# A hybrid encoder block on one core: FFN sums kept in PSUM, weights split once, a planner that ranks by due time

## The chip, the cores and the metric

The kernel runs on one core of one Trainium2 chip. The metric is device time in microseconds (us) of one execution, as a median of several runs. Five engines work side by side, each through its own list of instructions in order: PE (matmul; PEld is its weight load), DVE (elementwise and reductions), ACT (activations, copies), POOL (elementwise on SBUF) and SP, which here issues the DMA transfers.

## The reference

One layer with 1024 tokens of width 1024, in f32: a SwiGLU FFN of inner width 2816, a token mixer, and a second FFN, each behind an RMSNorm that a conditioning vector modulates.

```python
x = x + 0.5 * g1 * swiglu(mod1(rms(x)), w1, w3, w2)
h = mod2(rms(x))
z = h @ w_in        # 8 heads of forget attention (q,k,v), 8 sparse query heads, index scores, gates
ya = fox_attention(...)                  # causal softmax with a cumulated forget bias
yb = dsa_attention(...)                  # softmax over the 256 best keys of each query by the index scores
x = x + g2 * ((sigmoid(ga) * (ya @ w_br_fox) + sigmoid(gb) * (yb @ w_br_dsa)) @ w_out)
x = x + 0.5 * g3 * swiglu(mod3(rms(x)), w1', w3', w2')
```

## The kernel before

**Arithmetic.** Every f32 matrix is split into a rounded high part and a low remainder (`wh`, `wl` of a weight, made by an ACT copy and a DVE or POOL subtraction), and each block product is three matmuls (`mm3`, line 390): high by high, high by low, low by high. A matmul takes 128 rows by 128 columns of weights and up to 512 columns of data.

**The FFNs.** Each is computed by a scheme with seven block products in place of eight (quarters a11, a12, a21, a22 of a weight, b11 to b22 of the data, and sums s1 to s4 and t1 to t4 of them). In the way up, `UpPair` (line 1417) takes one of 11 pairs of 256 inner columns; `steps` runs seven products for m = 0 (w1) and m = 1 (w3), one per `yield`. `product` (1457) splits a weight, takes a PSUM bank of 512 columns, and issues 12 matmuls. The seven products are put together by DVE: tile `u` or `v` in SBUF plus the PSUM bank (`plus`, line 1475), 14 such adds a pair. Then come SiLU on ACT, the multiplication, the sums t1 to t4 of the result for the second half, and stores of seven operands to `d_g` in DRAM. `up_all` (1528) sets the order: the first products of `head` pairs, then pair after pair, and between steps loads, weight sums and the conditioning matrices (`extra`). In the way down, `Down` (1568) runs the seven products over 11 blocks each with four banks, reading `d_g` back; `out` (1624) adds banks to the residual `xc` with `add`, a DVE operation, with `u` as an intermediate sum. There are eight banks, all of one pool (`bank`, bufs=8).

**The middle.** After the first FFN come a projection with `w_a`, the index scores, the exact top-k by bisection on DVE and ACT, while PE projects with `w_f` (forget attention's q, k, v), `w_q` (sparse queries) and `w_g` (gates, first half of the tokens); then attention of 16 heads with the gates of the second half beside it. `load_w` (496) loads a weight to a raw tile `wr` and splits it: ACT writes `wh`, POOL writes `wl`. The gates' weights are loaded and split twice, once for each half of the tokens. `Ring` (477) turns a few raw tiles and pairs in two pools, and `Ahead` (980) loads some pieces ahead. Then `branches`, `mixer_out` and the second FFN follow.

**The planner.** Nearly all of it is issued through `Plan` (163). `take` records each operation as a task with its dependencies and a rank: the place in program order plus `behind`. `flush` (264) then places tasks: on each engine it looks at the first 60 waiting tasks in order of rank and takes the one that could start first (a later one only if it starts over 0.05 us earlier), with durations from `length` (246), a result counted as 0.12 us late, one DMA wire of 345 GB/s, and a lock between DVE and POOL where both read SBUF (`t.port`). The instructions are then issued in the order of these planned starts, so each engine's list is fixed before the run. Tiles take a slot of their pool when their first task is placed.

Of the kernel before, what the change touches and what calls it, by code (L numbers as in the profile page):

```python
# [161 lines left out]

class Plan:
# [18 lines left out]
    def take(self, engine, op, a, kw):  # L182
# [31 lines left out]
        for j in before:  # L214
            self.tasks[j].after.append(t)
        t.left = len(before)
# [6 lines left out]
        t.port = engine in ("vector", "gpsimd") and "accum_out" not in kw and not any(  # L223
            v.tile.pool.space == PSUM for v in reads + writes)
# [21 lines left out]
    def length(self, t, e):  # L246
        if e == "tensor":
            if t.exact:
                return max(0.08, t.n / 2250.0)
            if t.op == "transpose":  # L250
                return t.n / 860.0
            return max(0.24, t.n / 500.0)
        more = "accum_out" in t.kw
        if e == "scalar":
            return 0.1 + t.n / 1200.0 + (0.3 if more else 0.12 if any(isinstance(t.kw.get(x), View) for x in ("bias", "scale")) else 0.0)
        if e == "vector":
            if t.op == "tensor_tensor_scan":
                return 0.1 + t.n / 450.0
            return max(0.2, 0.08 + t.n / 960.0 + (0.18 if more else 0.06 if t.op == "scalar_tensor_tensor" else 0.0))
        if e == "gpsimd":  # L260
            return 0.1 + t.n / (900.0 if t.op == "tensor_scalar" else 440.0)
        return 0.35

    def flush(self, keep=()):
# [6 lines left out]
        waiting = {e: [] for e in self.ENGINES}  # L271

        def release(t):
            insort(waiting[t.engine], t, key=lambda u: u.rank)
# [28 lines left out]
        while len(order) < len(tasks):  # L303
# [20 lines left out]
            d = self.length(t, e)  # L324
            end = s + d + 0.12
# [24 lines left out]
            for u in t.after:  # L350
                u.left -= 1
                u.ready = max(u.ready, s + d if u.engine == e and e != "sync" else end)
                if not u.left:
                    release(u)
# [35 lines left out]
def mm3(k, out, w_hi, w_lo, m_hi, m_lo, start, stop):  # L390
    mm = k.nc.tensor.matmul
    mm(out, w_hi, m_hi, start=start, stop=False)
    mm(out, w_hi, m_lo, start=False, stop=False)
    mm(out, w_lo, m_hi, start=False, stop=stop)
# [82 lines left out]
class Ring:  # L477
# [7 lines left out]
    def raw(self):  # L485
        p, n = self.raws[self.j % len(self.raws)]
        self.j += 1
        return p.tile([128, D], F32, tag="wr", name="wr", bufs=n)
# [6 lines left out]

def load_w(k, src, n):

    nc = k.nc
    raw = k.w.raw()
# [916 lines left out]

class UpPair:


    def __init__(self, k, i, w13, wq, bank, d_g, any_):  # L1420
# [3 lines left out]
        self.ahead = []  # L1424
# [28 lines left out]
    def block(self, ps, w, b, c):  # L1453
        s = slice(c * 128, c * 128 + 128)
        mm3(self.k, ps, w[0][:, s], w[1][:, s], *self.k.B[b][c], c == 0, c == 3)

    def product(self, src, b):
        w, ps = self.weight(src), self.bank()
        for c in range(4):
            self.block(ps, w, b, c)  # L1460
# [9 lines left out]
    def steps(self):  # L1470

        nc, tile, product, store = self.k.nc, self.tile, self.product, self.store
        u, v, z, g = [None, None], [None, None], {}, {}

        def plus(out, ps, t):
            nc.vector.tensor_add(out, ps, t)
            return out

        def result(m, j, t):

            if m == 0:
                z[j] = t
                nc.scalar.activation(t, t, AF.Silu)
            else:
                self.any.tensor_mul(t, t, z[j])
                g[j] = t
                if j != "b12":
                    store(j, t)
# [39 lines left out]
def up_all(k, pairs, head, order, steps, ahead, extra, eng, again=False, every=lambda n: n % 8):  # L1528
# [12 lines left out]
    for i, n in order:  # L1541
# [18 lines left out]
        if i >= 2 and len(order) - k.up_step < (PAIRS - 2) * 14 and every(k.up_step):  # L1560
            nc.behind = 150
            next(extra, None)
            nc.behind = 0
    stores(True)
# [3 lines left out]
class Down:  # L1568
# [5 lines left out]
             ("a21", "t1", None), ("a12", "b22", None))  # L1574
    LEAD = 6

    def __init__(self, k, s, w2, wq, bank, d_g, homes, x_in, done, any_):
        self.k, self.s, self.w2, self.wq, self.bank, self.d_g, self.done = k, s, w2, wq, bank, d_g, done
        self.a = {n: [None] * PAIRS for n in ("a11", "a12", "a21", "a22", "s2")}
        self.g, self.u, self.loaded = {}, {}, 0  # L1580
# [8 lines left out]
    def loads(self, upto):  # L1589

        while self.loaded < min(upto, 7 * PAIRS):
# [5 lines left out]
            for n, m in {0: [(q - 5, 0)] if q >= 5 else [], 2: [(q, 1)], 3: [(4 + q, 1), (4 + q, 0)]}.get(p, []):  # L1597
                if n < (4 if p < 3 else 8):
# [25 lines left out]
    def out(self, p, d, ps):  # L1624
# [5 lines left out]
        if p == 0:  # L1630
            u[d] = t512(self.k, name="u")
            nc.scalar.activation(u[d], ps, AF.Copy)
            add(0, 0, d, u[d])
# [3 lines left out]
        elif p == 2:  # L1637
            nc.vector.tensor_add(u[d], ps, u[d])
            add(0, 1, d, u[d])
        elif p == 3:  # L1640
            nc.vector.tensor_add(u[d], ps, u[d])
            add(1, 1, d, u[d])
            add(1, 0, d, u[d])
# [3 lines left out]
        elif p == 5:  # L1647
            add(0, 1, d, ps)
            add(1, 1, d, ps)
# [5 lines left out]
    def run(self, steps={}):  # L1655

        k = self.k
        for p, (first, _, early) in enumerate(self.ORDER):
            ps = [self.bank() for _ in range(4)]
# [619 lines left out]
```

## Time and profile before

| What | Value |
|---|---|
| runs before | 2259.95, 2266.53, 2271.02 us (median 2266.53) |
| profiled execution: span | 2259.4 us, 0.55 us under the fastest of the runs |
| busy: PE, DVE, ACT, POOL | 96%, 80%, 49%, 12% of the span |
| DMA | 315.89 MB, mean 140 GB/s |
| mean clock granted to PE | 0.989 of full |

The stages, by the names of the tiles in the trace: the first FFN's way up to about 479 us, its way down to about 708, the `w_a` projection to 746, index scores to 850, projections beside top-k to 1046, attention from 1052 to 1418, branches and output projection from 1428, the second FFN's products from about 1625 to the end. A busy PE in a profile contains the pipelined end of each matmul, so whether it runs at its pace is better read from the number of matmuls in a stretch than from its share of busy time.

### The profile page before, as it was taken

How to read it: one execution, taken by the hardware profiler on the slowest of the kernel's cores; microseconds unless marked ns; L12 is line 12 of the kernel's file. 1: busy time of each engine (PE TensorE's matmuls, PEld its weight loads, DVE VectorE, ACT ScalarE, POOL GpSimd, SP SyncE). 2: the span in 40 equal slices, each digit the busy share in tenths (PEclk: the TensorE clock that was granted, in tenths of full speed). 3: DMA queues.
4: the chain of work that ended last, by engine and by line, in shares of the span. 5: the costliest groups of instructions: out<-in, count | busy, mean ns of one | idle time of the engine just before them, and what ended most of it. 6: DMA issues, size and time to landing. Idle time of an engine off the chain costs nothing.

```text
span 2259.4 us, 31187 instructions
## 1 busy us (share of the span) xinstructions
PE 2178.7 (96%) x10508; PEld 1799.5 (80%) x10508; DVE 1802.3 (80%) x3391; ACT 1101.8 (49%) x1996; POOL 268.6 (12%) x255
## 2 busy tenths in 40 slices
PE   7999999999999999998999999899999999999999
PEld 5777888787887989996778887687888888888887
DVE  7998987889775488888788877668898877769765
ACT  4432232344464476787687787423443333324443
POOL 0000000000010223323555433000000000000000
PEclk9999999999999999999999999999999999999999
DMA  9234554497421313334332210767223442258520
GB/s 336 81 114 161 168 173 131 146 367 238 126 74 61 121 61 122 113 122 136 107 110 89 76 35 20 278 239 256 87 80 131 135 133 96 93 179 319 168 75 38
DMA packets 187421, 315.89 MB, mean 140 GB/s; under 512 B 27366, under 2 KB 51942, under 8 KB 187260
## 3 DMA queue, kind: packets, MB, share of 16 engines
q1 hardware_dynamic: 187260, 313.89, 41.1%
q8 instruction: 83, 1.36, 0.2%
q14 instruction: 78, 0.64, 0.1%
HBM read 237.53 MB, written 76.28 MB: 139 GB/s over the span
## 4 chain that ended last, share of the span: by engine, by line
PE 45%; DVE 3%; ACT 2%; DMA 2%; issue 1%; SPq 0%; ACTq 0%; DVEq 0%; POOL 0%
PE b L358 34%; PE py L358 6%; PE pt L358 3%; PE p L358 2%; DVE macc L358 1%; DMA wr<-in_w_g 1%; DMA mraw<-in_ada_w 0%; ACT pth L358 0%; ACT pr L358 0%; DVE ptl L358 0%; ACT kst L358 0%; DVE qs L358 0%; DMA wr<-in_wbr 0%; ACT yt L358 0%; DVE kst L358 0%
## 5 line engine op out<-in xcount | busy, mean ns | idle before, releaser
L358 PE MATMUL b<-h,wh 128*128 128x512 f32 x2720 | 855.8, 396 | 10.0 <-ACT wh L358 5.0
L358 PEld LDWEIGHTS b<-h,wh 128*128 128x128 f32 x2720 | 511.9, 189 | 136.1 <-ACT wh L358 9.1
L358 PE MATMUL b<-h,wl 128*128 128x512 f32 x1360 | 533.7, 395 | 2.4 <-DVE wl L358 2.4
L358 ACT ACTIVATE wh<-wr 128x512 fp32r<-128x512 f32 (+2 forms) x368 | 245.5, 676 | 469.3 <-PE b L358 343.8
L358 PEld LDWEIGHTS b<-h,wl 128*128 128x128 f32 x1360 | 256.2, 188 | 64.2 <-DVE wl L358 4.2
L358 DVE TENSOR_TENSOR z<-b,z 128x512 f32<-128x512 f32 x308 | 207.3, 684 | 73.0 <-PE b L358 71.9
L358 PE MATMUL b<-wl,wh 128*128 128x512 f32 x616 | 241.8, 393 | 5.5 <-DVE wl L358 5.5
L358 PE MATMUL b<-wh 128*128 128x512 f32 x616 | 239.4, 391 | 2.5 <-ACT wh L358 1.7
L358 PE MATMUL b<-wh,wl 128*128 128x512 f32 x616 | 241.2, 392 | 0.0
L358 DVE TENSOR_TENSOR wl<-wr,wh 128x512 fp32r<-128x512 f32 x312 | 206.7, 683 | 32.9 <-ACT wh L358 32.8
L358 PE MATMUL pj<-wh,h 128*128 128x384 f32 (+1 forms) x768 | 179.5, 319 | 0.1
L358 ACT ACTIVATE wh<-a 128x512 fp32r<-128x512 f32 x132 | 83.3, 631 | 194.0 <-PE b L358 168.3
L358 POOL TENSOR_TENSOR wl<-wr,wh 128x1024 fp32r<-128x1024 f32 (+2 forms) x56 | 120.1, 2150 | 283.8 <-ACT wh L358 276.9
L358 DVE TENSOR_TENSOR wl<-a,wh 128x512 fp32r<-128x512 f32 x132 | 91.4, 693 | 76.8 <-ACT wh L358 76.8
L358 PEld LDWEIGHTS b<-wl,wh 128*128 128x128 f32 x616 | 116.6, 189 | 31.9 <-DVE wl L358 7.6
L358 PEld LDWEIGHTS b<-wh 128*128 128x128 f32 x616 | 116.1, 188 | 27.8 <-ACT wh L358 2.3
L358 PEld LDWEIGHTS b<-wh,wl 128*128 128x128 f32 x616 | 116.4, 189 | 24.6 <-DVE wl L358 0.4
L358 PEld LDWEIGHTS pj<-wh,h 128*128 128x128 f32 x768 | 132.4, 188 | 1.1 <-ACT wh L358 0.2
L358 DVE TENSOR_TENSOR z<-z 128x512 f32<-128x512 f32 x176 | 119.4, 690 | 10.7 <-DVE z L358 0.5
L358 PE MATMUL pj<-wl,h 128*128 128x384 f32 (+1 forms) x384 | 122.6, 319 | 0.5 <-POOL wl L358 0.5
L358 POOL TENSOR_SCALAR pr<-pr,mn 128x128 f32<-128x128 f32 (+7 forms) x128 | 101.2, 804 | 153.7 <-DVE mn L358 136.8
L358 DVE TENSOR_TENSOR wl<-g,wh 128x512 fp32r<-128x512 f32 x154 | 106.7, 695 | 0.0
(283 smaller groups left out, 3677.3 us busy)
## 6 DMA issues: line engine op xcount, KB each, us to landing
d_g<-z SPq DMA_DIRECT2D x154, 256.0 KB
g<-d_g SPq DMA_DIRECT2D x154, 256.0 KB
mraw<-in_ada_w SPq DMA_DIRECT2D x144, 256.0 KB
wr<-in_w13a SPq DMA_DIRECT2D x112, 256.0 KB
wr<-in_w13b SPq DMA_DIRECT2D x88, 256.0 KB
wr<-in_w_g SPq DMA_DIRECT2D x32, 512.0 KB
a<-in_w2a SPq DMA_DIRECT2D x44, 256.0 KB
a<-in_w2b SPq DMA_DIRECT2D x44, 256.0 KB
```

Of the source, the lines that this page charges most:

```text
L358: getattr(getattr(self.tc.nc, e), t.op)(*map(real, t.a), **{n: real(v) for n, v in t.kw.items()})
```

## The change

It has three parts and what goes with them.

1. **FFN sums in PSUM.** The eight banks become two pools of four: `b`, as before, and `y`. A product may be given a bank that already holds a sum (`product(src, b, ps)`): its first matmul then adds to what is there. Where a partial sum is needed twice, ACT copies the bank to a `y` bank (`seeded`). Four zero products at the start of each FFN (`seed_banks`) put the `y` banks in a state in which matmuls add. Pairs marked `early` (the first six of the first FFN, the third of the second) keep the first sum in SBUF as before and seed `y` from there later. `Down` works likewise: products 0, 1, 3, 4 on `b` banks ("x"), 2, 5, 6 on `y`, and the last blocks of products 0, 3, 5 and 6 are done bank by bank (`APART`). Residual tiles are loaded in another order.
2. **Weights split once.** `Pre` loads a piece of up to 512 columns of `w_f`, `w_q` and `w_g`, splits it on ACT and DVE, and stores both parts to DRAM, during the first FFN (one step of it after each `up_all` step from the third pair on, `behind` 20, and with each of the first 44 blocks of `Down`), through four tiles `p`. `load_w` then loads the two parts straight into `wh` and `wl`. The rings have no raw tiles, and six pairs in place of five. The first FFN's split weights turn in six pairs of tiles in place of eight.
3. **Due times.** New `deadlines` gives each task the latest time at which it is due: PE tasks at the sum of PE durations before them in rank order, others 20 us (`SLACK`) later, then backwards the least over those that wait for it or for its tile's slot. Waiting tasks are ordered by that in place of the rank. `length` has other durations, and for each engine its own delay of a result (0.23 us for PE, 0.16 ACT, 0.145 DVE, 0.105 POOL). `t.port` is set by the operation and the inputs in SBUF.

```diff
 def release(t):
-    insort(waiting[t.engine], t, key=lambda u: u.rank)
+    insort(waiting[t.engine], t, key=lambda u: u.due)
...
+    def deadlines(self):
...
+        for t in ordered:
+            t.len, t.lat = self.length(t, t.engine)
...
+            t.due = at + SLACK
+            if t.engine == "tensor":
+                t.due = at
+                at += t.len
...
+        for t in reversed(ordered):
+            d = t.due
+            for u in t.after:
+                d = min(d, u.due - t.len - (t.lat if u.engine != t.engine else 0.0) - (2.0 + t.bytes / 345e3 if t.engine == "sync" else 0.0))
+            for u in soft.get(t.pos, ()):
+                d = min(d, u.due - t.len - t.lat)
+            t.due = d
...
+class Pre:
+    def steps(self):
+        for c in range(0, self.n, H):
+            hi, lo = (t512(k, F32R, "pre", "pre")[:, :w] for _ in range(2))
+            nc.sync.dma_start(lo.bitcast(F32), self.src[:, c:c + w])
+            yield
+            nc.scalar.activation(hi, lo.bitcast(F32), AF.Copy)
+            nc.vector.tensor_sub(lo, lo.bitcast(F32), hi.bitcast(F32))
+            yield
+            for d, x in zip(self.parts, (hi, lo)):
+                nc.sync.dma_start(d[:, c:c + w], x.bitcast(F32))
...
 def load_w(k, src, n):
+    if isinstance(src, Pre):
+        hi, lo = k.w.pair()
+        for t, d in zip((hi, lo), src.parts):
+            nc.sync.dma_start(t[:, :n].bitcast(F32), d)
+        return hi, lo
...
+def seeded(k, src):
+    y = k.seed_bank()
+    k.nc.scalar.activation(y, src, AF.Copy)
+    return y
...
 # UpPair.steps
-            u[m] = tile()
-            nc.scalar.activation(u[m], product(self.a11[m], "b11"), AF.Copy)
+            x[m] = product(self.a11[m], "b11")
+            u[m] = copy(x[m]) if early, else y[m] = seeded(k, x[m])
-            result(m, "b11", plus(tile(), product(self.a12[m], "b21"), u[m]))
+            result(m, "b11", product(self.a12[m], "b21", x[m]))     # early: a DVE add as before
-            plus(u[m], product(self.s2[m], "t2"), u[m])
+            product(self.s2[m], "t2", y[m])
+            u[m] = copy(y[m])
-            v[m] = plus(tile(), product(self.a21[m], "t3"), u[m])
+            w[m] = product(self.a21[m], "t3")
-            ps = product(self.a11[m], "t1")
-            result(m, "b22", plus(tile(), ps, v[m]))
-            plus(u[m], ps, u[m])
+            product(self.a11[m], "t1", y[m])
+            result(m, "b22", plus(w[m], copy(y[m])))
-            result(m, "b21", plus(v[m], product(self.a22[m], "t4"), v[m]))
+            product(self.a22[m], "t4", w[m])
+            result(m, "b21", plus(w[m], u[m]))
-            result(m, "b12", plus(u[m], product(self.a12[m], "b22"), u[m]))
+            result(m, "b12", product(self.a12[m], "b22", y[m]))
...
 # Down
+    BANKS, APART = "xxyxxyy", {0: 2, 3: 2, 5: 2, 6: 3}
...
 # layer
-            k.wq = wq = Halves(k, pool(w0s, "w0", True, side="right"), 8, [nc.vector, nc.gpsimd])
+            k.wq = wq = Halves(k, pool(w0s, "w0", True, side="right"), 6, [nc.vector, nc.gpsimd])
-            bank = lambda: pp.tile([128, H], F32, tag="b", name="b", bufs=8)
+            bank = lambda: pp.tile([128, H], F32, tag="b", name="b", bufs=4)
...
-        k.w = Ring((w1, 3, 1), (w2, 2, 2))
+        k.w = Ring((w1, 3, 0), (w2, 3, 0))
```

In the diff of `UpPair.steps` the two branches of `early` are written in one line.

More of the change, by code (lines that the diff above doesn't have):

```diff
@@ L160, in real @@
     return v.real() if isinstance(v, View) else v
+SLACK = 20.0
 class Plan:
@@ L215, in take @@
             self.tasks[j].after.append(t)
+        t.waits = len({self.tasks[j].engine for j in before} - {engine})
         t.left = len(before)
@@ L222, in take @@
         t.bytes = 4 * int(np.prod(shape))
-        t.port = engine in ("vector", "gpsimd") and "accum_out" not in kw and not any(
-            v.tile.pool.space == PSUM for v in reads + writes)
+        wide = [v for v in reads if int(np.prod(v.shape[1:])) > 8]
+        sb = [v for v in wide if v.tile.pool.space != PSUM]
+        if engine == "gpsimd":
+            t.port = bool(sb)
+        elif engine == "vector":
+            if op in ("tensor_scalar", "tensor_copy", "reciprocal"):
+                t.port = len(sb) == 1 and "accum_out" not in kw and writes[0].tile.pool.space != PSUM
+            else:
+                t.port = len(sb) >= 2
+        else:
+            t.port = False
         if engine == "tensor":
@@ L262, in length @@
-        return 0.35
+            ap = sum(isinstance(t.kw.get(x), View) for x in ("bias", "scale"))
+            return 0.11 + n / 1200.0 + (0.1 if more else 0.0) + (0.06 if ap else 0.0), 0.16
+        if e == "gpsimd":
+            if t.op in ("tensor_scalar", "memset"):
+                return 0.08 + n / 960.0, 0.105
+            return 0.06 + n / 440.0, 0.105
+        if t.op == "tensor_tensor_scan":
+            d = 0.15 + n / 480.0
+        elif t.op == "tensor_tensor_reduce":
+            d = 0.17 + n / 960.0
+        elif t.op == "scalar_tensor_tensor" or more:
+            d = 0.13 + n / 960.0
+        elif t.op == "tensor_scalar" and t.port:
+            d = 0.075 + n / 1920.0
+        else:
+            d = 0.07 + n / 960.0
@@ L323, in flush @@
             s, t, e = best
-            d = self.length(t, e)
-            end = s + d + 0.12
+            d = t.len
+            end = s + d + t.lat
             if t.port:
@@ L351, in flush @@
                 u.left -= 1
-                u.ready = max(u.ready, s + d if u.engine == e and e != "sync" else end)
+                u.ready = max(u.ready, s + d + (0.1 if "accum_out" in t.kw else 0.0) if u.engine == e and e != "sync" else end)
                 if not u.left:
@@ L1414, with seed_banks @@
 OPERANDS = ("b11", "b21", "b22", "t1", "t2", "t3", "t4")
+def seed_banks(k, pool, z):
+    k.seed_bank = lambda: pool.tile([128, H], F32, tag="y", name="y", bufs=4)
+    for y in [k.seed_bank() for _ in range(4)]:
+        k.nc.tensor.matmul(y, z[:, 0:128], z, start=True, stop=True)
+def seeded(k, src):
+    y = k.seed_bank()
+    k.nc.scalar.activation(y, src, AF.Copy)
+    return y
 class UpPair:
@@ L1423, in __init__ @@
         self.run = self.steps()
-        self.ahead = []
+        self.ahead, self.early = [], False
     def load1(self, home="g", halves=(0, 1)):
@@ L1451, in weight, with product @@
         return self.ahead.pop(0) if self.ahead else self.wq.split(src)
[L1453 to L1458, printed above, removed]
+    def product(self, src, b, ps=None):
+        w = self.weight(src)
+        on = ps is not None
+        ps = ps if on else self.bank()
         for c in range(4):
-            self.block(ps, w, b, c)
+            s = slice(c * 128, c * 128 + 128)
+            mm3(self.k, ps, w[0][:, s], w[1][:, s], *self.k.B[b][c], c == 0 and not on, c == 3, skip_group_check=True)
         return ps
@@ L1470, in steps, with copy @@
     def steps(self):
[L1472 to L1477, printed above, removed]
+        k, nc, tile, product, store = self.k, self.k.nc, self.tile, self.product, self.store
+        x, y, w, u, q, z, g = ([None, None] for _ in range(5)), None, None, None, None, {}, {}
+        x, y, w, u, q = x
+        def copy(ps):
+            t = tile()
+            nc.scalar.activation(t, ps, AF.Copy)
+            return t
@@ L1525, in steps, with up_all @@
             yield
-def up_all(k, pairs, head, order, steps, ahead, extra, eng, again=False, every=lambda n: n % 8):
+def up_all(k, pairs, head, order, steps, ahead, extra, eng, again=False, every=lambda n: n % 8, pre=iter(())):
     nc = k.nc
@@ L1563, in up_all @@
             nc.behind = 0
+        if 2 <= i:
+            nc.behind = 20
+            next(pre, None)
+            nc.behind = 0
     stores(True)
@@ L1658, in run @@
         for p, (first, _, early) in enumerate(self.ORDER):
-            ps = [self.bank() for _ in range(4)]
+            kind = self.BANKS[p]
+            if kind == "y":
+                ps = self.y
+            elif p in (0, 3):
+                ps = [self.bank() for _ in range(4)]
+                x = ps
+            else:
+                ps = x
+            new = p in (0, 3)
             ops = []
@@ L1899, in layer @@
             pairs = [UpPair(k, i, w13a, wq, bank, d_g[0], nc.vector) for i in range(PAIRS)]
+            for q in pairs[:head]:
+                q.early = True
             ops = Operands(k, 0, x, nc.vector)
@@ L1946, in layer @@
             rest = side_by_side(ModHalf(k, i, h, bank).steps(d_row) for i in range(2, 6) for h in range(2))
+            pre = chain(*(w.steps() for g in (w_f[0], w_f[1], w_f[2], w_g[0:3], w_f[3], w_g[3:6], w_q[0], w_g[6:9], w_q[1], w_g[9:16]) for w in g))
             run = lambda i: [next(pairs[i].run) for _ in range(2)]
@@ L2028, in layer @@
             assert next(rest, None) is None
+            for _ in pre:
+                pass
             nc.flush([t for r in down.x for t in r] + [t for r in wa for t in r] + k.hh[0] + k.hl[0] + [a.acc for a in sq1])
@@ L2166, in layer @@
             pairs = [UpPair(k, i, w13b, wq, bank, d_g[1], nc.vector) for i in range(PAIRS)]
+            pairs[2].early = True
             def load_x(j):
```

141 lines of the change are left out of this document (102 added, 39 removed).

## The prediction

> **What bounds the kernel now.** I read the page's heads first, then the view by stretches of time (busy us and count of PE, weight loads, DVE, ACT and POOL, then the clock that PE was granted, the DMA share and GB/s).
>
> ```profile
> span 2259.4 us, 31187 instructions
> PE 2178.7 (96%) x10508; PEld 1799.5 (80%) x10508; DVE 1802.3 (80%) x3391; ACT 1101.8 (49%) x1996; POOL 268.6 (12%) x255
> ...
> 104.00:128.00 24.00, 22.73 (x86) 16.51 (x87) 23.90 (x40) 12.04 (x21) 0.00 (x0) 0.93 0.08 15
> 128.00:220.00 92.00, 91.52 (x393) 73.10 (x391) 83.45 (x155) 27.62 (x48) 0.50 (x2) 1.00 0.46 156
> 220.00:246.00 26.00, 21.49 (x83) 16.62 (x82) 23.15 (x38) 6.56 (x11) 0.00 (x0) 0.87 0.56 185
> 246.00:676.00 430.00, 426.10 (x1847) 343.84 (x1846) 362.75 (x590) 175.26 (x302) 9.26 (x8) 1.00 0.52 177
> 676.00:746.00 70.00, 64.47 (x309) 57.62 (x309) 33.63 (x62) 29.08 (x48) 5.26 (x4) 0.98 0.18 64
> 746.00:850.00 104.00, 97.05 (x565) 92.25 (x564) 78.00 (x126) 66.31 (x113) 24.02 (x21) 1.00 0.29 96
> 850.00:1046.00 196.00, 196.00 (x1128) 179.61 (x1127) 171.85 (x502) 149.52 (x275) 57.25 (x28) 1.00 0.35 119
> 1046.00:1070.00 24.00, 15.76 (x69) 12.76 (x67) 16.48 (x56) 15.92 (x27) 8.74 (x11) 0.86 0.45 153
> 1070.00:1418.00 348.00, 331.11 (x2078) 270.27 (x2078) 278.73 (x633) 260.35 (x557) 162.85 (x179) 0.99 0.23 72
> 1418.00:1428.00 10.00, 0.03 (x2) 0.02 (x1) 3.06 (x5) 3.52 (x7) 0.00 (x0) 0.69 0.68 216
> 1428.00:1525.00 97.00, 97.00 (x415) 79.28 (x416) 69.64 (x109) 32.41 (x54) 0.00 (x0) 0.98 0.79 277
> 1525.00:1546.00 21.00, 18.96 (x81) 14.03 (x79) 20.47 (x31) 8.81 (x16) 0.00 (x0) 1.00 0.96 331
> 1625.00:2045.00 420.00, 420.00 (x1816) 340.20 (x1815) 333.27 (x533) 146.76 (x240) 0.00 (x0) 1.00 0.37 125
> ```
>
> PE is the bound, and the change removes no product. The second FFN (1625 to 2045) shows the floor: 420 us over 1816 matmuls of 512 columns is 0.2313 us each, without a gap. So the DVE work that leaves that stage buys nothing there: DVE at 79% held nothing up. The top-k stage (850 to 1046) is also full. Only places where PE falls behind that pace can pay.
>
> First FFN, by that pace: 104 to 128 did 86 x 0.2313 = 19.9 us of work (4.1 lost), 220 to 246 did 19.2 (6.8 lost), 128 to 220 lost 1.1; the 430 us after them lost 430 - 1847 x 0.2313 = 2.8. For attention I need the shorter matmuls' pace, from the timeline (start, us, engine, operation), and the count by form, first and last of 16 rows.
>
> ```profile
> 1411.41 0.28 PE L358 MATMUL py<-pth,vst 128*128 128x256 f32 x1
> 1411.53 0.28 PE L358 MATMUL py<-ptl,vst 128*64 128x256 f32 x1
> 1412.17 1.04 PE L358 MATMUL pt<-ident,pr 128*128 128x128 f32 x8
> ...
> L358 PE MATMUL py<-h,wh 128*128 128x512 f32 x256 | 90.6, 412 | 1.4 <-ACT wh L358 1.3
> ...
> L358 PE MATMUL pt<-ident,nat 128*64 128x128 f32 x8 | 1.7, 271 | 0.0
> ```
>
> 256 columns take about 0.117 from start to start, an f32 transpose (1.04 - 0.27)/7 = 0.109. Widths between, on a line through 0.117 and 0.231: 384 at 0.174, 448 at 0.203, 320 at 0.146. From 1052 to 1418 the sixteen rows hold 480 of 512 columns (111 us), 672 of 256 (79), 672 transposes (73), 96, 64 and 64 of 384, 448 and 320 (39), and 96 short ones (about 5): 307 us of 366. Some 58 us are lost there, the largest sum in the kernel. The stage from 676 to 746 lost about 6, that from 746 to 850 about 12 (same paces).
>
> **The change, part by part.**
>
> *Order by due time.* DVE's order at 221 shows what it would mend.
>
> ```profile
> 221.22 3.47 DVE L358 TENSOR_TENSOR z<-z 128x512 f32<-128x512 f32 x5
> 224.60 1.28 DVE L358 TENSOR_TENSOR wr<-wr,s 128x512 f32<-128x512 f32 x2
> 226.09 1.65 PE L358 MATMUL b<-h,wh 128*128 128x512 f32 x3 [3.81 <-ACT wh L358]
> 104.15 2.33 PE L358 MATMUL b<-h,wh 128*128 128x512 f32 x4 [2.74 <-ACT h L358]
> ```
>
> Five sums that are only stored (t1 to t4 for the second half) go before the weight sums that PE waits 3.81 us for. Ranked by due time, the stored ones come last. The 10.9 us of both places include the half clock that follows (0.93 and 0.87 in their stretches against 1.00). I take 8 of 10.9; bounds 0 and 11. The Trainium skill, "TensorE: Matmul & The Clock Gate", Part 1, has the clock halved only behind an idle window of about 3.4 us; by that rule the wait of 2.74 at 104 would cost no clock, and my 8 would be about 7. The trace has 0.93 in that stretch, so it is not followed.
>
> In attention PE's own waits are short.
>
> ```profile
> PE py L358 <- ACT pth L358: 4.1, 8, 1.5
> PE py L358 <- DVE ptl L358: 3.2, 10, 0.3
> ...
> 1052.39 1.94 PE L358 MATMUL pt<-ident,nat 128*128 128x128 f32 x8 [5.89 <-issue]
> 1421.01 5.65 DMA wr<-in_wbr
> ```
>
> No engine is full (DVE 278.73 of 348, ACT 260.35), so order and latency set it, and the planner's costs change just there: matmul results 0.23 us late instead of 0.12. Bounds: all 58 come back (850 to 1046 runs full); or the gate products, the only free filler, are used up sooner and more of the end runs unfilled, 20 us more at the rate lost from 1046 to 1070 (8.2 of 24): +7. I take -22, nearer the middle row (1070 to 1418) than either end, because the PV chain pth, ptl, product stays serial. The two handovers (5.89 at 1052, 10 us at 1418) wait for pools and DMA that nobody moves: 0, bounds -4 to +4. Index stage (746 to 850): -3 of 12, bounds -8 to +3; 676 to 746: -3, bounds -5 to +4 because four instead of eight banks serve the products, and the spread norm holds one of them.
>
> *Products summed in PSUM.*
>
> ```profile
> L358 DVE TENSOR_TENSOR z<-b,z 128x512 f32<-128x512 f32 x308 | 207.3, 684 | 73.0 <-PE b L358 71.9
> L358 ACT ACTIVATE z<-b 128x512 f32<-128x512 f32 x44 | 25.6, 586 | 12.0 <-PE b L358 10.6 <-DVE z L358 1.1
> L358 ACT ACTIVATE wh<-wr 128x512 fp32r<-128x512 f32 x320 | 198.4, 629 | 426.7 <-PE b L358 343.8 <-DVE wr L358 31.9 <-issue 20.5
> ```
>
> A pair had 14 DVE adds from PSUM and has 4 (6 where early): 98 fewer in the first FFN, 108 in the second, x 0.684 = 67 and 74 us; the down products drop 20 more each (14 us). ACT gains 56 and 46 copies and 8 per down pass, x 0.586 = 37 and 32 us. Both hide under PE; without that cover they would be +37 and +32. The two times four zero products (8 x 0.23 = 1.8 us) fall into 0 to 12 and 1418 to 1428, where PE idles. What is new is that PE waits: t4 adds onto bank w only after ACT has copied y and DVE has added it to w, while one product passes, 12 x 0.2313 = 2.78 us. ACT 0.59 plus DVE 0.68 fit; even one other instruction ahead on each (0.63 + 0.68) makes 2.58. Behind two more, PE waits 0.5 or so. There are 44 such places (11 pairs x 2 x 2). Bounds 0 and 44 x 0.7 = 31; I take +5, near zero because DVE goes from 86% (104 to 676) to 80% and the second FFN from 79% to about 62%.
>
> *Weights split once.*
>
> ```profile
> L358 POOL TENSOR_TENSOR wl<-wr,wh 128x1024 fp32r<-128x1024 f32 (+2 forms) x56 | 120.1, 2150 | 283.8 <-ACT wh L358 276.9
> L358 ACT ACTIVATE wh<-wr 128x1024 fp32r<-128x1024 f32 x32 | 33.9, 1060 | 23.2 <-issue 8.6 <-DMA wr<-in_w_g 6.1 <-PE pj L358 4.7
> L358 ACT ACTIVATE wh<-wr 128x768 fp32r<-128x768 f32 x16 | 13.2, 849 | 19.4 <-DMA wr<-in_w_f 18.6 <-PE pj L358 0.8
> ...
> wr<-in_w_g SPq DMA_DIRECT2D x32, 512.0 KB
> ...
> wr<-in_w_f SPq DMA_DIRECT2D x16, 384.0 KB
> ...
> wr<-in_w_q SPq DMA_DIRECT2D x8, 256.0 KB
> ```
>
> Later stages lose 120 us of POOL and 13.2 + 33.9 + 8 x 0.63 = 52 us of ACT, already in the -22 and -3. The first FFN gains 56 pieces of 512 columns and 16 of 256: about 44 us of DVE and 41 of ACT, behind the FFN's own work (cover: DVE 80%, ACT about 53%; uncovered, +44). DMA: 16.8 MB read, 33.6 written there, on SP's queue: 246 to 676 moved 177 x 430 = 76 MB, with 50 more 294 GB/s. The row at 1525 shows 331 at a share of 0.96, so 345 at full: 85%. From 1428 to 1525 DMA ran at 277 with PE full: 0, bounds 0 and +10. Later loads double (25 MB more over 672 us, 37 GB/s on a share of 0.35 at most): 0. SP then issues 216 more transfers among the FFN's loads and stores; a store waiting on ACT and DVE holds the loads queued behind it, covered by loads issued some nine steps (25 us) ahead.
>
> Sum: -8 - 22 - 3 - 3 + 5 = -31, so 2228.4 against the profiled span of 2259.4. The runs were 2259.95 to 2271.02: the span lies 0.55 under the fastest and 7.1 under the median. Half of that on top gives 2232.
>
> **The rivals.** *Attention follows the plan:* it loses 28 of its 58 instead of 36, and the handovers and index stage give 12 more: another -32, 2200. For it: no engine above 85%. Against: the end (1375 on) has no filler.
> *Only the FFN stalls go:* without the -22 and one -3, 2257. For it: the 0.2 to 0.6 us breaks are engine latency that no order removes.
> *PE waits on the PSUM chain, slower:* at 44 places; it decides from 47/44 = 1.1 us each, when it eats the 36 us of gain and 11 more; at 1.4 (two more instructions on each engine) it is +62 for the +5, 2289. Against: due time puts exactly these first.
> *The clock drops:* short PE breaks between banks cost clock in both FFNs, 0.93 as at 104 to 128: 7% of 992 us (104 to 676 and 1625 to 2045), +69, 2301. The Trainium skill, same page, section "A second HAM failure mode: psum-queue depth-cycling", describes such an oscillation. Against: attention is full of short breaks and keeps 0.99.
>
> **How the numbers follow.** Chances: 0.50 the forecast (own range 2212 to 2252), 0.21 attention follows the plan, 0.13 only the FFN stalls, 0.09 the chain, 0.03 the clock, 0.04 the first FFN's DMA or split work (the +10 and part of the +44 over the third case, 2270 to 2285). Half a per cent, 11 us, is about what a measurement here can tell. Faster 0.74 (the first two and 0.03 of the third), same 0.12 (the rest of it and half of the last), slower 0.14. The range 2185 to 2272 leaves out 0.05 below and 0.14 above.
>
> **What would show it.** Right: no PE wait above 2 us from 100 to 250; the busy count 1052 to 1418 in some 345 us; no wl on POOL there; 1816 matmuls in 420 us of the second up pass still; DMA above 0.8 from 250 to 650. Wrong: PE waiting on DVE z or ACT z in either FFN by tens of us, clock under 0.98 there, or attention as long as now.

## The result, and the profile after

The changed kernel took 2227.43 us (median of 4 runs, 2226.87 to 2228.6) against 2265.0 for the kernel before beside it: 0.9836 of it, 95% interval 0.9815 to 0.9856. The forecast was 2232. The profiled execution took 2227.29 with a span of 2225.6, so 33.8 us of span went. That the total came out as forecast is luck: the terms for the order, for the sums in PSUM and for the weights split once were each wrong by 9 us or more, and the errors cancelled.

The page's head, changed kernel:

```profile
span 2225.6 us, 31413 instructions
PE 2165.1 (97%) x10516; PEld 1799.3 (81%) x10516; DVE 1649.4 (74%) x3217; ACT 1147.4 (52%) x2130; POOL 151.5 (7%) x201
...
DMA packets 226589, 391.40 MB, mean 176 GB/s; under 512 B 31718, under 2 KB 62438, under 8 KB 226428
```

DVE lost 153 us and POOL 117, ACT gained 46, and 75.5 MB of traffic came on top (75 worked out). The stretches that answer to those of before (same view: us, then busy us and count of PE, weight loads, DVE, ACT and POOL, granted clock, DMA share, GB/s):

```profile
104.00:128.00 24.00, 20.96 (x91) 16.55 (x90) 23.93 (x40) 14.93 (x27) 0.00 (x0) 1.00 0.24 74
128.00:220.00 92.00, 89.22 (x379) 70.61 (x378) 73.69 (x141) 40.35 (x74) 2.43 (x2) 1.00 0.66 217
220.00:246.00 26.00, 25.75 (x110) 20.19 (x109) 20.02 (x34) 12.21 (x23) 0.00 (x0) 1.00 0.83 285
246.00:478.00 232.00, 227.64 (x975) 181.00 (x974) 175.32 (x287) 104.52 (x187) 0.00 (x0) 1.00 0.83 280
478.00:573.00 95.00, 87.77 (x375) 69.85 (x374) 83.91 (x140) 47.15 (x85) 0.00 (x0) 0.98 1.01 354
573.00:708.00 135.00, 132.30 (x588) 108.44 (x588) 100.24 (x164) 77.27 (x138) 9.90 (x8) 1.00 0.46 152
850.00:1046.00 196.00, 196.00 (x1128) 179.57 (x1127) 149.61 (x529) 139.95 (x266) 0.00 (x0) 1.00 0.56 188
1046.00:1388.00 342.00, 329.14 (x2145) 281.63 (x2143) 280.10 (x638) 253.14 (x553) 135.59 (x174) 0.99 0.34 105
1590.00:2010.00 420.00, 419.27 (x1814) 339.35 (x1813) 270.41 (x428) 166.26 (x286) 0.00 (x0) 1.00 0.37 126
```

Read by the count of matmuls at 0.2313 us: 104 to 128 now loses 3.0 us and 220 to 246 loses 0.6, 10.9 before. But 128 to 220 loses 4.3 (1.1 before), 246 to 478 loses 6.5 and 478 to 573 loses 8.3, where the 430 us from 246 had lost 2.8 in all. What the two stalls gave back was lost again beside them.

For the rest I cut each trace at the same events: the first product of the first FFN, the first of its way down, its last, the first projection, the last index operation, attention's first transpose, its last PV product, the first branch product, the second FFN's first product of the way down, the end. Lengths in us:

| kernel | up | down | `w_a` | index | top-k | attention | handover | branches, 2nd up | 2nd down |
|---|---|---|---|---|---|---|---|---|---|
| before | 451.2 | 227.5 | 40.1 | 98.0 | 208.0 | 365.6 | 10.0 | 616.6 | 210.9 |
| changed | 450.2 | 230.8 | 42.2 | 88.2 | 206.9 | 341.7 | 5.8 | 618.5 | 209.6 |
| planner only | 438.4 | 216.1 | 40.1 | 92.4 | 234.9 | 344.7 | 7.3 | 616.1 | 209.6 |
| no split once | 441.9 | 219.4 | 39.4 | 95.2 | 235.6 | 342.6 | 7.3 | 618.3 | 209.6 |
| no PSUM sums | 443.7 | 220.0 | 39.9 | 88.0 | 206.9 | 341.2 | 5.7 | 615.7 | 209.6 |
| rank order | 460.7 | 234.2 | 42.5 | 89.0 | 202.9 | 339.5 | 10.1 | 618.1 | 209.6 |
| old lengths | 450.8 | 230.1 | 43.2 | 89.4 | 207.1 | 350.1 | 5.3 | 619.1 | 209.6 |
| delay 0.12 | 459.0 | 229.5 | 42.7 | 87.4 | 204.8 | 350.4 | 6.5 | 617.4 | 209.6 |
| t4 own bank | 439.7 | 229.4 | 40.8 | 89.2 | 206.9 | 340.1 | 5.9 | 619.1 | 209.6 |
| sums up only | 450.0 | 214.4 | 39.9 | 88.9 | 206.9 | 342.1 | 5.1 | 619.3 | 209.6 |
| old planner | 452.2 | 236.1 | 43.0 | 91.5 | 202.0 | 355.3 | 9.6 | 618.1 | 209.6 |
| six pairs | 437.3 | 215.9 | 39.9 | 96.8 | 236.1 | 344.2 | 5.8 | 613.8 | 209.6 |
| transfers only | 444.1 | 213.2 | 40.1 | 89.8 | 206.9 | 345.4 | 7.4 | 614.2 | 209.6 |
| combined | 439.5 | 220.0 | 39.9 | 89.3 | 206.9 | 341.8 | 7.4 | 617.6 | 209.6 |

So most of the 33.8 us came from attention (23.9), index scores (9.8) and the handover (4.2); the first FFN took 2.3 us more than before.

Some work crosses these cuts, and two rows must be read with that. Of the 1544 projection matmuls (tile `pj`), 385 stood before the last index operation in the kernel before, 357 in the changed one: 28 matmuls of 384 columns (28 x 0.174 = 4.9 us) went from the index stage to top-k. Top-k is none the longer for it, because the 5.89 us that PE waited at its end are gone. And in the kernel before and in every kernel that sums in PSUM on the way down, 12 to 17 of the 192 matmuls of the `w_a` projection (3 us or so) run before the last product of the way down; in the others none do. Way down and `w_a` are therefore best compared together.

### The profile page after: what moved, and what is told of

Its sections match the earlier page's. It is cut to its first block, busy times and chain, and to the rows that moved or that the text cites. A ratio compares the mean times of both kernels' runs of the same rounds, so it can differ in the third digit from the quotient of the medians.

```text
span 2225.6 us, 31413 instructions
## 1 busy us (share of the span) xinstructions
PE 2165.1 (97%) x10516; PEld 1799.3 (81%) x10516; DVE 1649.4 (74%) x3217; ACT 1147.4 (52%) x2130; POOL 151.5 (7%) x201
## 4 chain that ended last, share of the span: by engine, by line
PE 78%; DMA 9%; DVE 6%; ACT 4%; issue 2%; SPq 1%; POOL 0%; DVEq 0%; ACTq 0%
PE b L434 37%; PE y L434 19%; PE pj L434 11%; PE py L434 6%; PE p L434 3%; PE pt L434 3%; DMA wr<-in_w13a 1%; DVE wl L434 1%; SPq L434 1%; DMA mraw<-in_ada_w 1%; DMA pre<-in_w_f 1%; DVE z L434 1%; DMA na<-d_na 1%; DMA d_g<-z 1%; DMA a<-in_w2a 0%
## 5 line engine op out<-in xcount | busy, mean ns | idle before, releaser
L434 PE MATMUL b<-h,wh 128*128 128x512 f32 x1664 | 524.0, 396 | 10.8 <-DVE z L434 6.9
L434 PEld LDWEIGHTS b<-h,wh 128*128 128x128 f32 x1664 | 311.3, 188 | 90.3 <-DVE z L434 12.2
L434 ACT ACTIVATE wh<-wr 128x512 fp32r<-128x512 f32 x312 | 195.5, 629 | 364.8 <-PE b L434 154.4
L434 PE MATMUL y<-h,wh 128*128 128x512 f32 x1056 | 332.0, 395 | 3.3 <-ACT z L434 3.0
L434 PE MATMUL b<-h,wl 128*128 128x512 f32 x832 | 327.3, 394 | 0.0
L434 PEld LDWEIGHTS y<-h,wh 128*128 128x128 f32 x1056 | 198.0, 188 | 51.5 <-ACT z L434 4.2
L434 PE MATMUL y<-h,wl 128*128 128x512 f32 x528 | 207.5, 393 | 0.0
L434 PE MATMUL b<-wh,wl 128*128 128x512 f32 x352 | 137.1, 389 | 0.0
L434 PE MATMUL b<-wl,wh 128*128 128x512 f32 x352 | 137.0, 389 | 0.0
L434 PE MATMUL y<-wh 128*128 128x512 f32 x264 | 104.1, 396 | 7.4 <-ACT wh L434 6.6
```

Source lines behind the costliest of these rows:

```text
L434: getattr(getattr(self.tc.nc, e), t.op)(*map(real, t.a), **{n: real(v) for n, v in t.kw.items()})
```

## The experiments

Times are medians; ratios stand against the kernel before, run on the same chip; its medians there were 2264.1 to 2265.7, so the runs can be set beside each other. The diffs are shortened, and lines that are no code say in words what was put back.

**1. The planner alone.** Sums and split weights as before.

```diff
-class UpPair / Down: sums in PSUM, two pools of four banks
+class UpPair / Down: as before, one pool of eight banks
-        w_f, w_q, w_g = Pre(...)
-        k.w = Ring((w1, 3, 0), (w2, 3, 0))
+        k.w = Ring((w1, 3, 1), (w2, 2, 2))
```

> The kernel before with the new planner alone (due times, new durations and delays); FFN sums on DVE and eight banks as before, weights split where they are used. Stage lengths before and after the change: first FFN with the w_a projection 718.8 and 723.2 us, index and top-k 306.0 and 295.0, attention 366.5 and 342.0, handover to the branches 10.1 and 5.5, the rest 827.5 and 828.1. If order makes the gain: attention 350 or less, total 2235 to 2245. If relief of POOL and ACT by the weights split once makes it: attention 360 or more, total 2258 or more.

2230.44 us, 0.9855 (0.9831 to 0.988): alone, this part gives nearly all that the change gives, and the total is some 5 us below the range expected of the order. Up and down of the first FFN take 24.2 us less, attention 20.9, but top-k 26.9 more. One stretch of the way up and one of the way down, first before, then the planner alone:

```profile
104.00:250.00 146.00, 139.74 (x575) 109.45 (x576) 134.40 (x237) 47.49 (x81) 0.50 (x2) 0.96 0.41 135
560.00:682.00 122.00, 116.72 (x519) 95.58 (x518) 95.16 (x154) 65.47 (x114) 9.88 (x8) 1.00 0.33 105
```

```profile
104.00:250.00 146.00, 144.91 (x615) 114.55 (x614) 136.96 (x245) 46.30 (x79) 0.50 (x2) 1.00 0.44 142
560.00:682.00 122.00, 121.33 (x544) 100.41 (x543) 94.44 (x154) 65.90 (x117) 10.60 (x8) 1.00 0.28 86
```

40 matmuls more (9.3 us) in the first stretch, and 25 more (5.8 us) in one that the prediction had not looked at. In top-k, PE's chain of waits (us, times, longest):

```profile
PE pj L434 <- ACT gt L434: 11.3, 3, 6.9
PE pt L434 <- issue: 4.8, 1, 4.8
PE pj L434 <- ACT qkv L434: 3.7, 1, 3.7
```

With weights split in place, the new order lets PE wait 19.8 us for ACT's `gt` and `qkv` copies and at the stage's end, and the clock granted from 880 to 940 is 0.90. These waits are absent wherever the weights are split once.

**2. No weights split once.** Planner and sums; eight pairs of split weights in the first FFN again.

```diff
-        w_f, w_q, w_g = Pre(...)
-        k.w = Ring((w1, 3, 0), (w2, 3, 0))
+        k.w = Ring((w1, 3, 1), (w2, 2, 2))
```

> The changed kernel without the weights split once (raw tiles and rings as before, eight split pairs in the first FFN); new planner and PSUM sums stay. If order makes the gain: total 2222 to 2235, attention below 350. If relief makes it: index and top-k back to 304 or more and attention to 360 or more, total 2255. For the first FFN: if the 50 MB of added transfers cost its 4 us, it falls to 712 or less; if the PSUM chain costs them, it stays at 720 or more.

2242.38 us, 0.9907 (0.9883 to 0.9932). Against run 1 the sums cost 11.9 us, without any transfer added; top-k again has 235.6. Neither expectation held whole: attention has its gain (342.6), as the order should give, but the total is 7 above that theory's range, with top-k 28 us longer than in the kernel before. The first FFN with `w_a` falls to 700.7, so the added transfers or the split work cost it something too.

**3. No sums in PSUM.** Planner and weights split once.

```diff
-class UpPair / Down: sums in PSUM, two pools of four banks
+class UpPair / Down: as before, one pool of eight banks
```

> The changed kernel with the FFN sums back on DVE and eight banks in one pool; planner and weights split once stay. If the PSUM sums only make room for the split work: the first FFN's DVE rises to over 90% and that stage to 735 or more, the second FFN does not change (within 2 us), total 2240 or more. If the PSUM chain costs more than the room is worth: first FFN 715 or less, total 2220 or less.

2206.36 us, 0.9752 (0.9723 to 0.9782): 21.1 us faster than the changed kernel, as expected if the chain costs more than the room is worth. The sums in PSUM are a loss of 6.5 us in the way up, 10.8 down, 2.3 in the `w_a` stage and 2.8 before the second way down, though they take 137 us of DVE work out (1786.5 to 1649.4). Against run 1, the weights split once give 28.0 in top-k and 4.4 in the index stage, and take 5.3 up and 3.9 down.

**4. Order by rank**, with the new durations and delays.

```diff
-            insort(waiting[t.engine], t, key=lambda u: u.due)
+            insort(waiting[t.engine], t, key=lambda u: u.rank)
```

> The changed kernel with waiting tasks ordered by rank as before; new durations and delays stay. If the order by due time makes the gain: attention 358 or more, total 2250 or more. If the truer durations and delays make it: attention 350 or less, total 2225 to 2235.

2239.14 us, 0.9892 (0.9867 to 0.9917). The order by due time is worth 10.5 us in the way up, 3.4 in the way down and 4.3 at the handover; attention does without it (339.5), as the second expectation had it, though the total is 4 above that one's range. Top-k is 4.0 shorter by rank, but that is work moved: 380 of the `pj` matmuls stand before the last index operation here, 357 in the changed kernel, 23 x 0.174 = 4.0. What rank order gains there lies in the index stage, which takes 0.8 us more with 4.0 us more of work.

**5. Old durations, delay and lock**, with the order by due time.

```diff
     def length(self, t, e):
-        ...                                   # new durations and delays
+        return self.length0(t, e), 0.12       # length0 and t.port as before
```

> The changed kernel with its due-time order, but with the old durations, the old 0.12 us delay of every result and the old lock. Theory A (the new durations and delays gave attention's 24 us, the order nothing): attention back to 358 to 368 us, total 2243 to 2256. Theory B (the order by due time gave them): attention 340 to 346, total 2224 to 2234. The first FFN's way up stays at 448 to 456 if the order alone gave its gain.

2236.49 us, 0.9873 (0.986 to 0.9887). Attention 350.1: between the two theories' numbers. The new durations and delays are worth 8.4 us there, a third of its gain; the way up did not need them (450.8).

**6. Delay 0.12 again**, with the new durations.

```diff
-            t.len, t.lat = self.length(t, t.engine)
+            t.len, t.lat = self.length(t, t.engine)[0], 0.12
```

> The changed kernel with its new durations, but each engine's result counted 0.12 us late again instead of 0.23, 0.16, 0.145 and 0.105. Theory A (the later matmul result, which the prediction named, gave attention its gain): attention 356 to 366 us, total 2240 to 2252. Theory B (the durations did it, those of short and f32 matmuls above all): attention 340 to 347, total 2224 to 2234.

2237.06 us, 0.9878 (0.9865 to 0.9892). Attention 350.4, between the two theories' ranges and 8.7 above the changed kernel. With the new durations in place those 8 us are the delays' doing; the new durations and lock without the delays give attention nothing (350.4 against run 5's 350.1). The new delays without the new durations were not run. New durations with the old delay also cost the way up 8.8 us (459.0).

**7. t4 on a bank of its own.**

```diff
-            product(self.a22[m], "t4", w[m])
-            result(m, "b21", plus(w[m], u[m]))
+            plus(w[m], u[m])
+            result(m, "b21", plus(product(self.a22[m], "t4"), u[m]))
```

> The changed kernel, but product t4 of each pair goes to a bank of its own, and DVE adds it to w plus u afterwards: 22 DVE adds more in each FFN, and no product waits behind ACT's copy of y and DVE's sum. Theory A (this wait is what the sums cost in the ways up): way up of the first FFN 443 to 446 us for 450.2, second FFN to its down products 616 for 618.5, total 2217 to 2222, and PE's wait on DVE z, 6.9 us before, under 1.5. Theory B (the cost lies in the four banks instead of eight, or in the transfers): no change, 2225 to 2231.

2215.42 us, 0.978 (0.9767 to 0.9794): 12.0 us under the changed kernel, more than theory A gave it, with 22 more DVE adds in each FFN, and a way up of 439.7. What it took away is seen in the changed kernel: PE's waits in the way up (us, times, longest), then one of them with DVE's list and ACT's ahead of it (start, us, engine, operation).

```profile
PE b L434 <- DVE z L434: 6.9, 9, 1.5
PE y L434 <- ACT z L434: 3.0, 1, 3.0
```

```profile
149.45 0.69 DVE L434 TENSOR_TENSOR s<-wr 128x512 f32<-128x512 f32 x1 [2.01 <-DMA wr<-in_w13a]
150.06 0.69 DVE L434 TENSOR_TENSOR wl<-wr,wh 128x512 fp32r<-128x512 f32 x1
150.66 0.69 DVE L434 TENSOR_TENSOR wr<-wr 128x512 f32<-128x512 f32 x1
151.26 0.69 DVE L434 TENSOR_TENSOR wl<-s,wh 128x512 fp32r<-128x512 f32 x1
151.86 0.69 DVE L434 TENSOR_TENSOR s<-wr 128x512 f32<-128x512 f32 x1
152.46 0.69 DVE L434 TENSOR_TENSOR z<-b,z 128x512 f32<-128x512 f32 x1
153.20 0.73 PE L434 MATMUL b<-h,wh 128*128 128x512 f32 x2 [1.23 <-DVE z L434]
150.26 0.63 ACT L434 ACTIVATE wh<-s 128x512 fp32r<-128x512 f32 x1 [1.64 <-DVE s L434]
150.80 0.58 ACT L434 ACTIVATE z<-y 128x512 f32<-128x512 f32 x1
```

ACT's copy of y (150.80, 0.58) is done at 151.4; w's sum (152.46) could have run then, but DVE has been idle 2.01 us for a transfer and works off weight sums and splits first. The copy itself is late by the same transfer: PE had finished y at 147.3, but ACT's list had the split of `s` in front, and DVE's sum `s` waited for the load. In run 7 the view of the waits reads:

```profile
PE b L434 <- ACT h L434: 1.8, 1, 1.8
PE y L434 <- ACT z L434: 1.4, 1, 1.4
PE b L434 <- ACT y L434: 0.8, 2, 0.6
PE b L434 <- DVE h L434: 0.3, 1, 0.3
```

No wait on DVE `z` is left. The waits that the view names fall from 12.3 us in all (three more, 2.4 us, are not shown) to 4.3; the other 2.5 of the 10.5 us lie in breaks too short for it. Without the chain the sums in PSUM make the way up 4.0 us shorter than run 3's. The second FFN did not move (619.1 for 618.5), against theory A's 616: with DVE at 64% there, the chain had cost nothing.

**8. Sums in the way up alone.** `Down` as before, its seven products on the two sets of four banks in turn.

```diff
-            ps = self.y if kind == "y" else ...
+            ps = [(self.bank, k.seed_bank)[p % 2]() for _ in range(4)]
 # out(): DVE adds with u, as before
```

> The changed kernel with the sums in PSUM in the ways up alone; the way down takes its two sets of four banks in turn and adds on DVE as before. Theory A (the sums cost each way its own): way down of the first FFN 219 to 222 us for 230.8, total 2213 to 2219. Theory B (the way down is slow for the transfers of the weights split once, whatever adds): way down 228 to 232, total 2225 to 2230.

2207.26 us, 0.9748 (0.9735 to 0.9761), 20.2 under the changed kernel; way down 214.4, both below theory A's ranges. Half of the changed kernel's loss there has one place. Its ACT list and PE's, then 20 us of the changed kernel and of run 8 by count:

```profile
535.42 0.63 ACT L434 ACTIVATE pre<-pre 128x512 fp32r<-128x512 f32 x1 [3.27 <-DMA pre<-in_w_g]
541.61 0.97 PE L434 MATMUL y<-wh 128*128 128x512 f32 x3 [1.32 <-ACT wh L434]
546.99 0.63 ACT L434 ACTIVATE wh<-s 128x512 fp32r<-128x512 f32 x1 [2.13 <-DVE s L434]
547.68 0.79 PE L434 MATMUL y<-wh 128*128 128x512 f32 x1 [3.03 <-ACT wh L434]
548.69 0.63 PE L434 MATMUL y<-wh 128*128 128x512 f32 x1
549.12 0.63 PE L434 MATMUL y<-wl,wh 128*128 128x512 f32 x1
554.23 0.50 PE L434 MATMUL y<-wh 128*128 128x512 f32 x1 [1.72 <-ACT wh L434]
554.57 0.39 PE L434 MATMUL y<-wl,wh 128*128 128x512 f32 x1
554.80 0.40 PE L434 MATMUL y<-wh 128*128 128x512 f32 x1
```

```profile
537.00:557.00 20.00, 13.94 (x53) 9.65 (x51) 19.16 (x33) 11.35 (x21) 0.00 (x0) 0.91 1.01 338
```

```profile
538.00:558.00 20.00, 20.00 (x89) 16.52 (x88) 19.78 (x33) 12.92 (x24) 0.00 (x0) 1.00 0.99 343
```

ACT stands 3.27 us behind a late piece of `w_g`, then has squares of the residual and splits to catch up with; the longest of PE's three waits goes through DVE, whose weight sum `s` ACT waits 2.13 us for. That makes 36 matmuls fewer than run 8 (8.3 us), at the same full DMA. Of the other 8 us, some 3 are the 17 matmuls of `w_a` moved in, and some 3 are breaks from 676 to 684, where PE waits 1.67 us for ACT's `h` and 0.85 for its copy `u`. Run 8 has those squares and splits too, without the stall. The six kernels with sums on the way down and the weights split once take 229.4 us or more there, the four that split once but add on DVE there 220.0 or less. So the new way down brings the stall; but run 8 also puts back the residual's order of loading and drops most of the products that end bank by bank, so which of these does it is not shown.

**9. The old planner with both other parts.**

```diff
-            insort(waiting[t.engine], t, key=lambda u: u.due)
+            insort(waiting[t.engine], t, key=lambda u: u.rank)
 # and the diff of 5: old length(), 0.12, old t.port
```

> The changed kernel (sums in PSUM, weights split once) with the old planner entirely: order by rank, old durations, old delays. Theory A (what was left of attention's gain without the new durations, 15.5 us of 24, is the order by due time): attention 360 to 368 us, total 2262 to 2275, near the kernel before. Theory B (that rest is the 52 us of ACT and 120 us of POOL that the weights split once take out of the later stages): attention 347 to 353, total 2246 to 2256. The way up of the first FFN comes out at 465 to 475 either way, the top-k stage at 200 to 208.

2250.64 us, 0.994 (0.992 to 0.996). Attention 355.3, two us above theory B's range, which the total met: without the planner the weights split once give 10.3 of attention's 23.9. That is 120 us of POOL and 52 of ACT less in the later stages, and six pairs for five; the two were not told apart. Order by due time adds 5.2 (355.3 to 350.1), the delays the last 8.4. They overlap: the planner alone gave 20.9 (run 1), and with the new delays rank order does as well as due time (run 4). The way up, 452.2, is far from the 465 that I gave it. The handover is long again (9.6).

**10. Six pairs of split weights instead of eight**, on run 1.

```diff
-            k.wq = wq = Halves(..., 8, [nc.vector, nc.gpsimd])
+            k.wq = wq = Halves(..., 6, [nc.vector, nc.gpsimd])
```

> The planner alone (2230.4 us) with six pairs of split weights in the first FFN instead of eight, as the changed kernel has it to make room for the pieces split once. Theory A (the fewer pairs are what the weights split once cost there): way up 443 to 446 us for 438.4, way down 218 to 221 for 216.1, total 2236 to 2242. Theory B (transfers or split work cost it): 437 to 440 and 215 to 217, total 2228 to 2233.

2230.56 us, 0.9852 (0.9832 to 0.9873), run 1's time. The pairs cost nothing (437.3, 215.9).

**11. The transfers of the weights split once, without the split**, on run 3.

```diff
-            nc.scalar.activation(hi, lo.bitcast(F32), AF.Copy)
-            nc.vector.tensor_sub(lo, lo.bitcast(F32), hi.bitcast(F32))
-            for d, x in zip(self.parts, (hi, lo)):
+            for d, x in zip(self.parts, (lo, lo)):
```

> The kernel without sums in PSUM, its weights split once with the transfers as they were, but without the split itself: each piece is loaded to one tile and stored twice as it is, without ACT's copy and DVE's subtraction (about 41 and 44 us of work left out). Theory A (the transfers cost the first FFN its 9 us): way up 442 to 445 for 443.7, way down 218 to 221 for 220.0, total 2203 to 2208. Theory B (the split work on ACT and DVE costs it): 437 to 440 and 215 to 217, total 2195 to 2200.

2201.2 us, 0.9722 (0.9702 to 0.9743), 5.2 under run 3. The outcome is mixed: the way up keeps its loss (444.1 against run 10's 437.3: 6.8 us of transfers, as theory A had it), the way down drops to 213.2, even below theory B's range. The way up's loss has one place:

```profile
211.69 0.75 DVE L434 SCALAR_TENSOR_TENSOR macc<-mraw,cond,macc 128x512 f32<-128x512 f32 x1 [1.95 <-DMA mraw<-in_ada_w]
214.09 0.75 DVE L434 SCALAR_TENSOR_TENSOR macc<-mraw,cond,macc 128x512 f32<-128x512 f32 x1 [1.04 <-DMA mraw<-in_ada_w]
216.22 1.22 PE L434 MATMUL b<-h,wh 128*128 128x512 f32 x2 [3.89 <-ACT wh L434]
```

DVE waits for two late loads of the conditioning matrix; the weight sum that PE's next weight is made of stands behind them (214.76), PE waits 3.89 us and then runs at half pace until 222. SP's queue had stood 11.2 us behind a store of `z`, until 202, and then had pieces to issue between those loads; in run 10, without the pieces, it stood 11.8 us too and PE had no such wait. Run 8 does the split work in full and has a way down of 214.4, so that work need not cost it anything; whether a stall falls into the full stretch decides.

**12. Combined:** runs 7 and 8, and top-k ordered by rank.

```diff
-            insort(waiting[t.engine], t, key=lambda u: u.due)
+            insort(waiting[t.engine], t, key=lambda u: u.rank if self.by_rank else u.due)   # by_rank: top-k only
 # and the diffs of 7 and 8
```

> The changed kernel with t4 on a bank of its own (12.0 us off the total before), the way down adding on DVE with its two sets of banks in turn (20.2 off), and the top-k stage ordered by rank (4.0 shorter there). If the three add up: 2227.4 - 12.0 - 20.2 - 4.0 = 2191, range 2188 to 2197, below every kernel so far. If t4's DVE adds and the way down's meet on DVE, or a later due time shifts the loads: 2200 to 2206, no better than without sums in PSUM.

2205.92 us, 0.9742 (0.9721 to 0.9763): level with runs 3 and 8, 21.5 under the changed kernel, and 15 above the sum of the three gains. The way up keeps run 7's gain (439.5). Top-k stays at 206.9, which fits: run 4's gain was in the index stage, which this run orders by due time. The way down is 220.0 where run 8 had 214.4, by one stall:

```profile
573.69 0.63 ACT L434 ACTIVATE wh<-g 128x512 fp32r<-128x512 f32 x1 [5.00 <-DMA g<-d_g]
574.37 1.20 PE L434 MATMUL y<-wh 128*128 128x512 f32 x4 [3.40 <-ACT wh L434]
...
567.00:587.00 20.00, 16.60 (x66) 12.80 (x65) 16.80 (x28) 7.41 (x14) 0.00 (x0) 0.91 0.89 302
```

ACT stood 5.00 us for a load of `g`, PE waited 3.40 and ran at half pace behind it: 66 matmuls for run 8's usual 89, 5.3 us.

## Why the prediction was right in sum and wrong in its terms

**Order in the first FFN, -8: too small.** The stalls at 104 and 220 went, as forecast (7.3 us by count). But the planner alone took 24.2 us out of this FFN. I had costed only two stretches in which a wait stood out and counted the rest as nearly full; the stretch from 560 to 682 alone held 5.8 us more. The 2.8 us for 246 to 676 were too few because 16 of the 1847 matmuls counted there at full width were short (8 of one column, 8 of 128), so the loss was nearer 6, and the longest wait of that stretch's end, 3.20 us for DVE `wl` at 681.39, lay just behind its edge. The order itself accounts for 13.9 of it beside the other parts (run 4 against the changed kernel).

**Products summed in PSUM, +5: the step that failed.** It cost 21.1 us (run 3). The price was inside the bounds (0 to 31), and the place was named rightly for the way up: t4 behind ACT's copy and DVE's sum. What failed is "near zero because DVE goes from 86% (104 to 676) to 80%": a mean of 80% says nothing of the queue in front of one sum. At 152 DVE had five instructions there after a late transfer, and ACT's copy was held up by the same transfer. Run 7 prices the chain at 10.5 us for the 22 places of the first FFN, 0.48 each on average (nine of them show a wait), and at nothing in the second, where DVE's share is 64%. The prediction had no term for the way down, the larger half: with `w_a`, the sums cost 2.6 us there while DMA has room (run 2 against run 1) and 10.3 to 18.7 beside the split's transfers (run 12 against 7, run 8 against the changed kernel). The second FFN's 2.8 us is not explained.

**Weights split once, 0 in the first FFN: wrong by 9 us (the bounds were 0 and +10), and 0 in top-k: wrong by 28 the other way.** The forecast of 294 GB/s was a mean over 430 us. The page of before had the peak in its slices of 56.5 us, at 452 to 508:

```profile
DMA  9234554497421313334332210767223442258520
GB/s 336 81 114 161 168 173 131 146 367 238 126 74 61 121 61 122 113 122 136 107 110 89 76 35 20 278 239 256 87 80 131 135 133 96 93 179 319 168 75 38
```

At 367 there was little room where `Down` begins and goes on carrying pieces, and DMA is now full for 95 us (share 1.01 from 478 to 573; 0.67 from there to 650, not above 0.8 as I had written). The cover "loads issued some nine steps (25 us) ahead" was short for the conditioning's loads in run 11 and for one load of `g` in run 12. In top-k, that the stage is full and has nothing to gain held for the old planner only: the new one loses 27 us there unless the weights come ready. The two cancel in the changed kernel, and that interaction was in none of the rivals.

**Attention, -22: right in size (23.9), half right in reason.** The delay of 0.23 us that the prediction named is worth 8 to 9; the weights split once give 10 without the planner, and the order 5 without the delays and nothing beside them: each partly does the other's work.

**Handovers, 0: -4.2 and -5.9.** The prediction said that nobody moves what they wait for. The wait of 5.89 us before attention is gone in every kernel with the weights split once, and in none of the three others with the new planner (4.8 to 7.6 us). At the one behind attention the order by due time is what tells: by rank the wait is 9.6 to 10.1 us in three kernels, by due time 5.1 to 7.4 in the others. PE's waits at that place, before and changed:

```profile
PE b L358 <- ACT yh L358: 10.0, 1, 10.0
```

```profile
PE b L434 <- ACT wh L434: 4.1, 1, 4.1
```

The split of y is no longer last; a weight is late next.

**Index stage, -3: -9.8**, of which the planner alone gives 5.6 and the split once 4.4 (run 3 against run 1); but 4.9 of the 9.8 are the matmuls moved to top-k, so what it really lost less is some 5. **676 to 746, -3: +2.1**; not for the four banks, which the prediction had as the bound: run 8 has them and 39.9. With the new planner, kernels that add on DVE on the way down have 39.9 to 40.1. Those that sum in PSUM there have moved 13 to 17 of this stage's matmuls into the way down and still take 39.4 to 43.2, because PE waits at the stage's start for the residual's squares:

```profile
PE b L434 <- DVE nacc L434: 2.5, 1, 2.5
```

This line is the changed kernel's; run 2 has 2.3 and still takes only 39.4. What makes the rest beside the weights split once is not shown.

Of the signs set down: POOL writes no `wl`, the second way up does 1814 matmuls in 420 us, attention takes 342; one wait above 2 us stood between 100 and 250 after all (`y` for ACT's `z`, 3.0). The rival "PE waits on the PSUM chain" had the right mechanism at a third of its price, and it did not decide because the planner's gain in the same FFN was three times what I gave it.

## What to carry to other kernels

Summing in PSUM took work off DVE here but made TensorE wait on DVE's queue: cost such a chain by what stands ahead of the one instruction in that list, and ahead of the copy it needs, not by the engine's share. Place added transfers by the busiest slice of the stage, not by its mean. And time each part of a change alone and left out: here one part was a 21 us loss hidden behind the gains of the two others.

## What the runs showed of the hardware

A wait of 3.03 us left PE at half pace for some 3 us after it (starts 0.43 apart at 548.69 and 549.12), one of 1.72 did not (0.23 apart at 554.57 and 554.80). By the Trainium skill, "TensorE: Matmul & The Clock Gate", Part 1, the clock falls after an idle window of about 3.4 us; the trace has it fall behind a shorter one, as at 104 before. The length of the wait alone does not decide: in the changed kernel a wait of 3.04 us before 118.99 cost no clock (1.00 from 104 to 128, matmuls 0.23 apart), and in the kernel before one of 1.74 us before 553.42 was followed by some 3 us at half pace (starts 0.43 apart at 555.75 and 556.18). What decides is not shown.

With one core at work, DMA moved more than I took for full (345 GB/s). Run 3, the way down's first stretch:

```profile
471.00:566.00 95.00, 92.05 (x398) 72.91 (x396) 90.36 (x153) 53.44 (x95) 0.00 (x0) 1.00 1.03 373
```

The Trainium skill, "DMA: Bandwidth & Descriptors", Specifications, gives a limit of about 358 GB/s of HBM for each core, half of what a stack gives its two; 373 over 95 us, with the one core, is above that half.
